# A two-layer hybrid decoder trunk: SBUF buffers moved to 2 KB multiples, inputs laid out before the launch, the inverse's products alternated

## The chip, the cores and the metric

The kernel runs on one core of one Trainium2 chip. Its time is device microseconds, from one launch; the runs of a kernel are given by their median. Each core has TensorE (PE in the profile, its weight loads as PEld), VectorE (DVE), ScalarE (ACT), GpSimd (POOL), SyncE (SP, which only issues DMAs here) and 16 DMA engines. [...]

## The reference

256 positions of width 2048 go through two layers. Each layer normalises its input, projects it to 7692 columns, feeds three mixers from them and projects their gated outputs back:

```python
h = rms_norm(x, norm_w[l])                       # (256, 2048)
u = h @ w_in[l]                                  # (2048, 7692), float32
y_conv = conformer_conv(...)                     # 512 wide: GLU, 31-tap conv, LayerNorm, swish, 512 x 512
y_gdn  = gated_deltanet(...)                     # 6 heads of 128: 4-tap conv, chunked delta rule
y_att  = dilated_attention(...)                  # 12 heads of 64
x = x + concat(gated y_conv, y_gdn, y_att) @ w_out[l]
```

A last RMSNorm gives the output. All parameters are float32, and the result must be close to float32 accuracy. The delta rule needs, for each head and chunk, the inverse of a unit lower-triangular matrix (`triangular_solve` of the reference).

## The kernel before

**Products in three terms.** Weights and activations are split into a high part in float32r (a cheaper float32 for TensorE) and the low rest, and each product is high·high + low·high + high·low. For the weights ACT copies `raw` to `whi` and DVE subtracts to get `wlo`; for the activations `HT[0]` and `HT[1]` are the two parts of the transposed normalised input, each 16 blocks of 128 x 256, and `YT[0]`, `YT[1]` those of the mixers' outputs. `unit` (L453) issues the three products of one block. A matmul loads 128 columns of one operand as weights and streams the other one past them: with `chan` the weights are the stationary operand and 256 columns of `HT` or `YT` stream; otherwise 384 to 512 columns of `whi` or `wlo` stream. `last_unit` (L462) is used for the last 256 output columns, where `YT` is stationary and `HT`, which then holds weights, streams.

**Order.** The kernel is written as tasks; `Plan.run` gives each step a cost and an earliest start, and writes every engine's instructions in the order of its own model. On the chip each engine keeps that order. `load_weights` is one stream of chunks on SP's queue (two 128-row blocks of weights for each, four `raw` buffers, three `whi` and three `wlo`), `split_weights` follows, and `project` runs the jobs one after the other on two pairs of PSUM banks (`ACC`). Everything else of the mixers is put between the units of the projections.

**The start.** `load_x` loads `x` by columns between the first weight chunks (`X_BEFORE`); `norm_block`, `norm_half` and `norm_128` transpose each 128 x 128 piece on TensorE (32 transposes, L230) and split the result out of PSUM into `HT`. `square_sums` has ACT form the sums of squares of the same pieces; `finish_norm` makes 1/rms of them, which the evacuation of the projections applies, so the first products do not wait for it. `setup` loads small parameters as rows and turns them by TensorE transposes too (`turn`, L339): four for each layer.

**The inverse.** `inverse` inverts 32 x 32 blocks on DVE and then merges them: 12 products of 32 x 32 for each of several steps, then 64 x 64 ones, all plain float32 (L223; such a product shows as two matmul records in the profile). Each step's result is copied out of PSUM by DVE before the next step reads it. The two halves of the 128 partitions, named by `prs`, go through the steps one after the other, and so do the two groups of six heads in the 64 x 64 steps. The planner puts units of a projection between the steps.

**Placement.** In the built program `HT` and `YT` start 128 bytes past a multiple of 2 KB in each partition; `raw`, `whi` and `wlo` start 1856 bytes past one, and their second blocks of 384 columns 1344 bytes past one.

## Time and profile before

| | us |
|---|---|
| median of 3 runs | 997.62 |
| lowest and highest run | 996.41, 998.58 |
| the profiled execution | 998.17 |
| its span, first to last instruction | 996.5 |
| TensorE busy in the span | 983.1 (99%) |
| VectorE busy | 749.7 (75%) |
| ScalarE busy | 551.9 (55%) |
| GpSimd busy | 48.6 (5%) |

The granted clock was 0.997 of the higher level over the whole span. The profiled execution is 0.55 us above the median. A busy TensorE is not TensorE at its peak: matmuls overlap, so what one costs is read from how many start in a stretch (the pitch), not from the duration of one, and the waits show where it stood still. The chain of work that ended last follows, step by step, what released each instruction; its pieces give a start, a length and a count, and the length over the count is the pitch.

### The profile page before, as it was taken

What the parts mean: (1) busy time and instruction counts of PE and PEld (TensorE: products, weight loads), DVE (VectorE), ACT (ScalarE), POOL (GpSimd) and SP (SyncE); (2) the same over time, 40 slices, a digit from 0 to 9 for tenths busy, and PEclk for the clock granted to TensorE, in tenths of its full rate; (3) what the DMA queues carried; (4) which work ended last, traced back from release to release, by engine and by line L of the source; (5) the groups of instructions that cost most, each with busy time, mean ns of one, the idle gap of its engine ahead of it and who ended that gap; (6) DMA issues with size and microseconds to landing.
All of it is one profiled execution on the core that took longest, in us unless ns stands there. A gap on an engine that the chain in (4) does not pass through costs nothing.

```text
span 996.5 us, 19159 instructions
## 1 busy us (share of the span) xinstructions
PE 983.1 (99%) x7299; PEld 958.3 (96%) x7299; DVE 749.7 (75%) x1511; ACT 551.9 (55%) x1085; POOL 48.6 (5%) x70
## 2 busy tenths in 40 slices
PE   8999999999999999999999999999999999999996
PEld 7999999999999989999899999999999999999996
DVE  6587699988899666655557767999888987666672
ACT  7665345544676674454455633554447777545452
POOL 1000200200010000000000020002000101000000
PEclk9999999999999999999999999999999999999998
DMA  8665566644444635776766655666444456466772
GB/s 269 172 213 174 158 182 184 195 147 129 143 144 143 190 117 169 219 223 223 231 183 182 201 167 171 182 184 189 137 141 130 142 174 207 122 185 219 226 247 87
DMA packets 116585, 176.91 MB, mean 178 GB/s; under 512 B 8458, under 2 KB 97356, under 8 KB 116492
## 3 DMA queue, kind: packets, MB, share of 16 engines
q1 hardware_dynamic: 114572, 171.88, 56.4%
q0 software_dynamic: 1632, 3.02, 1.2%
q8 instruction: 57, 0.93, 0.4%
q10 hardware_dynamic: 288, 0.79, 0.2%
q14 instruction: 36, 0.29, 0.1%
HBM read 170.67 MB, written 4.98 MB: 176 GB/s over the span
## 4 chain that ended last, share of the span: by engine, by line
PE 97%; issue 1%; DMA 1%; DVE 0%; ACT 0%; SPq 0%; POOLq 0%; POOL 0%; DVEq 0%; ACTq 0%
PE acc L453 86%; PE mix L223 6%; PE mix L230 3%; DMA b<-in_x 1%; PE acc L462 1%; PE mix L751 0%; DVE wlo L190 0%; ACT b L182 0%; SPq L408 0%; DVE b L197 0%; SPq L390 0%; PE mix L339 0%; ACT whi L182 0%; POOLq L1300 0%; POOL rstd L239 0%
## 5 line engine op out<-in xcount | busy, mean ns | idle before, releaser
L182 ACT ACTIVATE whi<-raw 128x768 fp32r<-128x768 f32 (+4 forms) x389 | 339.7, 873 | 375.5 <-PE acc L453 319.0
L190 DVE TENSOR_TENSOR wlo<-raw,whi 128x768 fp32r<-128x768 f32 (+4 forms) x389 | 385.5, 991 | 193.0 <-ACT whi L182 186.2
L453 PE MATMUL acc<-HT,whi 128*128 128x256 f32 x2304 | 413.2, 281 | 0.0
L453 PEld LDWEIGHTS acc<-HT,whi 128*128 128x128 f32 x2304 | 352.0, 188 | 1.6 <-issue 1.5
L453 PE MATMUL acc<-HT,wlo 128*128 128x256 f32 x1152 | 321.7, 279 | 0.0
L453 PE MATMUL acc<-whi,HT 128*128 128x384 f32 (+1 forms) x1024 | 271.2, 346 | 0.0
L453 PEld LDWEIGHTS acc<-HT,wlo 128*128 128x128 f32 x1152 | 216.0, 188 | 0.0
L453 PEld LDWEIGHTS acc<-whi,HT 128*128 128x128 f32 x1024 | 179.8, 188 | 1.9 <-issue 1.0
L453 PE MATMUL acc<-wlo,HT 128*128 128x384 f32 (+1 forms) x512 | 172.6, 337 | 0.0
L453 PE MATMUL acc<-whi,YT 128*128 128x384 f32 (+2 forms) x640 | 162.8, 338 | 0.0
L453 PEld LDWEIGHTS acc<-whi,YT 128*128 128x128 f32 x640 | 114.2, 187 | 3.0 <-ACT whi L182 0.2
L453 PE MATMUL acc<-wlo,YT 128*128 128x384 f32 (+2 forms) x320 | 107.9, 337 | 0.4 <-DVE wlo L190 0.4
L187 DVE SCALAR_TENSOR_TENSOR b<-b,dw,b 128x255 f32<-128x255 f32 (+29 forms) x240 | 104.3, 461 | 0.2
L453 PEld LDWEIGHTS acc<-wlo,HT 128*128 128x128 f32 x512 | 96.1, 188 | 0.0
L453 PEld LDWEIGHTS acc<-wlo,YT 128*128 128x128 f32 x320 | 60.0, 187 | 2.2 <-DVE wlo L190 0.7
L230 PE MATMUL mix<-ident,b 128*128 128x128 f32 x312 | 51.2, 276 | 3.0 <-DMA b<-in_x 2.6
L182 ACT ACTIVATE b<-mix 128x256 f32<-128x256 f32 (+3 forms) x95 | 38.6, 422 | 19.1 <-PE mix L223 10.0
L187 DVE SCALAR_TENSOR_TENSOR b<-b,cw,b 128x255 f32<-128x255 f32 (+2 forms) x108 | 48.6, 473 | 0.0
L223 PE MATMUL mix<-b,b 128*128 128x128 f32 (+5 forms) x456 | 47.8, 285 | 0.4 <-ACT b L182 0.4
L230 PEld LDWEIGHTS mix<-ident,b 128*128 128x128 f32 x312 | 37.7, 140 | 8.3 <-DMA b<-in_x 3.5
L223 PEld LDWEIGHTS mix<-b,b 128*128 128x128 f32 (+3 forms) x456 | 38.0, 161 | 7.5 <-issue 2.7
L187 DVE SCALAR_TENSOR_TENSOR b<-b,b 128x256 f32<-128x256 f32 (+3 forms) x62 | 31.3, 510 | 2.7 <-ACT b L182 2.6
(149 smaller groups left out, 648.0 us busy)
## 6 DMA issues: line engine op xcount, KB each, us to landing
raw<-in_w_in SPq DMA_DIRECT2D x240, 384.0 KB, 3.1
raw<-in_w_in SPq DMA_DIRECT2D x48, 512.0 KB, 3.5
raw<-in_w_out SPq DMA_DIRECT2D x64, 384.0 KB, 3.8
raw<-in_w_out SPq DMA_DIRECT2D x12, 512.0 KB, 5.4
raw<-in_w_in SPq DMA_DIRECT2D x15, 396.0 KB, 4.6
raw<-in_conf_pw_w SPq DMA_DIRECT2D x4, 512.0 KB, 3.7
raw<-in_w_out SPq DMA_DIRECT2D x8, 256.0 KB, 4.2
b<-in_x SPq DMA_DIRECT2D x6, 256.0 KB
```

The costliest lines, as they stand in the source:

```text
L182: lambda: nc.scalar.activation(out_, in_, func, bias=bias, scale=scale, **kw))
L187: lambda: nc.vector.scalar_tensor_tensor(out_, a, s, b, op0=op0, op1=op1))
L190: return ("dve", 70 + _free(out_) / 0.96, lambda: nc.vector.tensor_tensor(out_, a, b, op=op))
L223: nc.tensor.matmul(o, a, b, start=f[0], stop=f[1])
L230: nc.tensor.transpose(o, a, ident)
L453: nc.tensor.matmul(o, w, m, start=first and i == 0 and not (chan and t % 2), stop=last and i == 2, skip_group_check=chan)
L462: nc.tensor.matmul(acc[t][:, :n], YT[w][:, k, s], HT[m][:, k, :n], start=k == 0 and i == 0, stop=k == KB - 1 and i == 2)
```

## The change

Four edits come together.

- **Inputs laid out before the launch.** `w_in`, `conf_pw_w` and `w_out` are stored so that the two 128-row blocks of a chunk lie side by side: each partition's part of a chunk of 384 columns is one run of 3072 bytes and no longer two of 1536. A transposed copy of `x` (`x_t`) is added beside `x`. All small parameters come as one 128 x 237 array for each layer (`params`), with channels on partitions.
- **The start.** `load_xt` and `norm_xt` read `x_t` and split it straight into `HT`, without transposes; `load_x` still loads `x`, now in eight pieces behind chunks 8 to 15, and for `square_sums` alone. `setup` becomes one DMA (on ACT's queue for layer 0, on SP's for layer 1), one activation and two small DVE steps.
- **The inverse.** The two `prs` halves of a 32 x 32 step are issued in one group, alternating; the second 64 x 64 product of one group of heads alternates with the first of the other.
- **Placement.** `lncs` and `ropes` and two pads (`PAD`) are allocated so that `HT`, `YT`, `PTs`, `raw`, `whi`, `wlo` and the 1024-wide buffers start on multiples of 2 KB; the 768-wide ones alternate between 0 and 1024 bytes past one. The residues of all slices that the projections use are then multiples of 512 bytes.

```diff
+PAD = (32, 16)
+    lncs = cp.tile([128, 384], F32, name="lncs")
+    ropes = cp.tile([128, NT, 32], F32, name="ropes")
+    cp.tile([128, PAD[0]], F32, name="pad0")
     HT = [cp.tile([128, KB, S], F32R, name=f"HT{i}") for i in range(2)]
...
+    cp.tile([128, PAD[1]], F32, name="pad1")
     HALF = [cp.tile([128, NT], F32, name=f"half{l}") for l in range(DEPTH)]
...
-    X_PIECES = [(256 * i, 256) for i in range(4)] + [(1024, 512), (1536, 512)]
-    X_BEFORE = {0: 0, 2: 1, 3: 2, 4: 3, 5: 4, 7: 5}
+    X_PIECES = [(256 * i, 256) for i in range(8)]
+    XT_BEFORE = {0: (0, 1), 1: (1, 1), **{i: (2 * i - 2, 2) for i in range(2, 9)}}
+    X_BEFORE = {8 + j: j for j in range(len(X_PIECES))}
...
-        yield from turn(MISC[l][:, 0:16], [(col(norm_w), 16)], cost=0.0 if l == 0 else 100.0)
+        yield ("dma", 200.0 if l else 0.0, lambda: (nc.sync if l else nc.scalar).dma_start(PAR[l], params[l]))
         yield ("set", misc_ready[l])
...
+    def load_xt(k0, m):
+
+        buf = yield ("get", S768)
+        yield ("dma", 128 * m * S * 4 / 330.0, lambda: nc.sync.dma_start(
+            buf[:, :m * S], bass.AP(tensor=x_t.tensor, offset=x_t.offset + k0 * S, ap=[[KB * S, 128], [1, m * S]])))
+        plan.spawn(norm_xt(k0, m, buf), 2)
+
+    def norm_xt(k0, m, buf):
+        yield ("wait", misc_ready[0])
+        for b in range(m):
+            k = k0 + b
+            yield from split(HT[0][:, k, :], HT[1][:, k, :], buf[:, b * S:(b + 1) * S], PAR[0][:, k:k + 1])
+            yield ("set", h_ready[0][k])
+        yield ("put", S768, [buf])
...
-            for p, (a, b) in enumerate(prs):
-                yield mms(*((psx[b, hc * 32:hc * 32 + 32], Lh(hc)[a, b], T3[a, hc, :]) for hc in range(HC)))
+            yield mms(*((psx[b, hc * 32:hc * 32 + 32], Lh(hc)[a, b], T3[a, hc, :]) for hc in range(HC) for a, b in prs))
...
+            yield mms(*(m for hc in range(HC) for m in third(hc)))
...
+            yield mms(*(down(0, j) for j in range(H)))
+            yield cpy(Xs[b, hs[0], :], h3(psx[b, :H * 64], 64))
+            yield mms(*(m for j in range(H) for m in (down(1, j), up(0, j))))
```

What this moves. On TensorE at the program's start, before (`mix` and `acc` are PSUM, `b` the loaded `x` or parameters):

```order
L309 MATMUL mix_118<-ident,ones 128x128 x10
L339 MATMUL mix_121<-ident,b_0_110 128x16
L230 MATMUL mix_120<-ident,b_0_85 128x128 x2
L309 MATMUL mix_119<-ident,ones 128x128 x5
L230 MATMUL mix_120<-ident,b_0_85 128x128 x2
L230 MATMUL mix_118<-ident,b_1_86 128x128 x4
L453 MATMUL acc_122<-whi_79,HT_71 128x396
L453 MATMUL acc_122<-whi_79,HT_72 128x396
```

And of the change:

```order
L316 MATMUL mix_121<-ident,ones 128x128 x10
L316 MATMUL mix_122<-ident,ones 128x128 x5
L453 MATMUL acc_125<-whi_82,HT_74 128x396
L453 MATMUL acc_125<-whi_82,HT_75 128x396
L453 MATMUL acc_125<-wlo_85,HT_74 128x396
```

The products of the first job now follow the 15 warm-up transposes at once; the transposes of `b` are gone here and between the later units of that job.

On ACT where the second copy of `x` is read (the last block of `HT`, then squares into `JUNK`, each with a copy of a weight chunk between), of the change:

```order
L191 ACTIVATE JUNK,ssq_153<-b_9_97 128x256 x2
L191 ACTIVATE whi_84<-raw_78 128x792
L191 ACTIVATE HT_74<-b_8_96,par_147 128x256
L191 ACTIVATE JUNK,ssq_153<-b_10_98 128x256 x2
L191 ACTIVATE whi_82<-raw_79 128x768
L191 ACTIVATE JUNK,ssq_153<-b_11_99 128x256 x2
L191 ACTIVATE whi_83<-raw_80 128x768
```

One pair of squares of 256 columns stands before each weight chunk, eight times; before, squares of 256 and 512 columns stood there in twelve single steps.

On TensorE in the inverse of layer 0, before (one step of the 32 x 32 merge and the two that follow):

```order
L223 MATMUL mix_119<-b_1_105,b_9_94 32x32 x6
L223 MATMUL mix_119<-b_1_105,b_11_96 32x32 x6
...
L223 MATMUL mix_118<-b_0_104,inv_115 32x32 x12
L223 MATMUL mix_118<-inv_115,b_0_104 32x32 x12
```

And of the change:

```order
L232 MATMUL mix_124<-b_1_108,b_9_97 32x32 x12
L232 MATMUL mix_124<-b_1_108,b_8_96 32x32 x12
...
L232 MATMUL mix_122<-b_0_107,inv_118 32x32 x2
L232 MATMUL mix_122<-inv_118,b_0_107 32x32
L232 MATMUL mix_122<-b_0_107,inv_118 32x32 x2
L232 MATMUL mix_122<-inv_118,b_0_107 32x32
```

A layer's 60 small products of 32 x 32 stand in two groups instead of four, and its 24 of 64 x 64 in three instead of four, with other partitions in turn inside a group.

## Rows read from the trace of the kernel before

**Rows 1.** Page, part 1: busy us, share of the span and instructions of each engine.
```profile
PE 983.1 (99%) x7299; PEld 958.3 (96%) x7299; DVE 749.7 (75%) x1511; ACT 551.9 (55%) x1085; POOL 48.6 (5%) x70
```

**Rows 2.** Waits of TensorE, the longest: us in total, times, longest us.
```profile
PE mix L230 <- DMA b<-in_x: 2.6, 2, 1.7
```

**Rows 3.** The chain in pieces: start us, length us, what, count.
```profile
100.46 43.11 PE acc L453 x366
143.79 6.13 PE acc L453 x54
...
429.25 16.97 PE acc L453 x96
446.88 16.64 PE acc L453 x96
...
977.06 5.75 PE acc L462 x48
```

**Rows 4.** Page, part 2: granted clock of TensorE in 40 slices, in tenths.
```profile
PEclk9999999999999999999999999999999999999998
```

**Rows 5.** TensorE's instructions by shape: count | busy us, mean ns.
```profile
L453 PE MATMUL acc<-HT,whi 128*128 128x256 f32 x2304 | 413.2, 281 | 0.0
...
L453 PE MATMUL acc<-whi,HT 128*128 128x384 f32 x896 | 237.0, 345 | 0.0
...
L453 PE MATMUL acc<-whi,YT 128*128 128x384 f32 x512 | 131.7, 338 | 0.0
```

**Rows 6.** Instructions of the first 11 us: start us, length us, engine, what.
```profile
0.80 0.43 SPq L390 DMA_DIRECT2D b<-in_x  x1
...
3.91 0.28 PE L339 MATMUL mix<-ident,b 16*128 16x16 f32 x1
...
4.84 0.53 ACT L182 ACTIVATE whi<-raw 128x396 fp32r<-128x396 f32 x1 [0.42 <-DMA raw<-in_w_in]
...
7.74 0.61 PE L453 MATMUL acc<-whi,HT 128*128 128x396 f32 x2
...
10.13 0.98 DVE L190 TENSOR_TENSOR wlo<-raw,whi 128x792 fp32r<-128x792 f32 x1 [0.36 <-ACT whi L182]
```

**Rows 7.** Stretches of 4 us; the last three: clock, DMA share, GB/s.
```profile
4.00:8.00 4.00, 2.32 (x15) 2.04 (x16) 2.26 (x5) 2.09 (x5) 0.13 (x1) 1.00 0.84 253
8.00:12.00 4.00, 3.04 (x18) 2.41 (x18) 1.87 (x4) 2.61 (x5) 0.00 (x0) 1.00 1.04 365
```

**Rows 8.** The chain in the first 30 us, columns as in rows 3.
```profile
12.40 2.17 PE acc L453 x12
14.57 0.87 PE mix L230 x8
...
29.44 0.11 PE mix L339
```

**Rows 9.** ACT's squares and weight copies after the first job's products: start, length.
```profile
22.50 0.42 ACT L182 ACTIVATE JUNK<-b 128x256 bf16<-128x256 f32 x1
22.82 0.19 ACT L182 ACTIVATION_READ_ACCUMULATOR JUNK<-b 128x1 f32 x1
...
25.46 0.83 ACT L182 ACTIVATE whi<-raw 128x768 fp32r<-128x768 f32 x1
```

**Rows 10.** The chain in layer 0's inverse, columns as in rows 3.
```profile
209.75 0.87 PE mix L223 x24
210.62 2.28 PE acc L453 x12
212.89 1.53 PE mix L223 x48
...
224.35 0.84 PE mix L223 x12
```

**Rows 11.** TensorE inside that inverse: start us, length us, what, count.
```profile
213.48 0.21 PE L223 MATMUL mix<-inv,b 32*32 32x32 f32 x1
...
213.60 0.82 PE L223 MATMUL mix<-inv,b 32*32 32x32 f32 x21
```

## The prediction

> **What bounds the kernel now.** I read the page's busy times first, then TensorE's waits, then the pieces of the chain. TensorE is busy 983.1 us, 99% of the span [rows 1], and its largest wait is 2.6 us in all, for pieces of `x` [rows 2]. The other engines wait for it. So an edit is worth what it takes off TensorE's own stream, and nothing else unless a cover breaks.

> What the stream costs is its pitch. 366 products of 256 columns take 43.11 us, 117.8 ns each; 54 others, of the same tiles and the same shape, take 6.13 us, 113.5 ns each; the 48 of the last job, also 256 columns, take 5.75 us, 119.8 ns each [rows 3]. For 384 columns two neighbouring stretches give 176.8 and 173.3 ns [rows 3]. [...] The 2304 products of 256 columns with `whi` go with half as many with `wlo`, 3456 in all, and the 896 and 512 of 384 columns with 704, 2112 in all [rows 5]. At 117.8 ns and at 175 ns (the middle of the two) they are 407 and 370 us, 777 of 996.5. One ns of pitch on all of them is 5.6 us; that is the size of what the placement can do either way.

> **The change part by part.**

> **The start.** Before, the first product starts at 7.74 [rows 6], and the first job's 96 products of 396 columns end where the transpose at 29.44 stands [rows 8]. Twelve of them take 2.17 us, 180.8 ns each [rows 8], so 96 need 17.4 us; the other 4.3 us after 7.74 are the 28 transposes of `x` that stand between them (8 take 0.87 us, 108.75 ns each [rows 8], so 3.0) and 1.3 us of stops. After: `x_t` is first on SP's queue. Before, the first `x` was issued at 0.80, and what SP issued right after it, `norm_w`, was turned by TensorE at 3.91 [rows 6]; `params` leaves on ACT's queue at the time of the first `x`. So ACT's split of block 0 can start near 4.1; `raw`, which landed by 4.84 [rows 6] and is now issued one place earlier, is copied behind it in 0.53 us [rows 6], and the first product stands at about 5.2. Two blocks last 12 x 0.181 = 2.2 us, to 7.4. The next pair of blocks needs 1.46 MB to have come in all (0.12 of parameters, 0.13 + 0.20 twice, 0.26 + 0.41), which at 253 to 365 GB/s [rows 7] from about 2.0 us is 6.0 to 7.8; with two splits, a copy and 0.98 us of DVE [rows 6] TensorE stops for about 1.5 us. From there a pair takes 0.67 MB, 1.8 us at 365 GB/s, against 2.2 us of products, and TensorE no longer waits. The job ends at 5.2 + 17.4 + 1.5 = 24.1 instead of 29.4: 5.3 less; I take **5.0**, with bounds 3.5 (the transposes alone, with four of them before 7.74) and 6.5 (no stop).

> **The parameters.** Of eight `setup` transposes two stand in that stretch; the six others cost 0.11 us of chain each [rows 8]: **0.7**. The two scaled copies on DVE are a few tenths of a us, and DVE is busy 75%: they are covered.

> **The second copy of `x`.** 2.1 MB more go over SP's queue behind chunks 8 to 15; each chunk with its piece is 0.66 MB, 1.8 us at 365 GB/s [rows 7], against 18 x 117.8 ns = 2.12 us of products. SP issues each piece ahead of a weight chunk, so the chunk queued behind it is what could be late. ACT has to do 0.83 us of copy and two squares of 0.42 + 0.19 us [rows 9], 2.05 us for the same 2.12. Both covers are thin but the three `whi` buffers lie ahead; cost nothing, and 8 x 0.2 = 1.6 us if ACT falls 0.2 us behind each time. 1/rms comes later than before, but nothing needs it until the third job asks for the first one's banks, about 17 us of products after the first job's end.

> **The weights' layout.** TensorE waits for no weight transfer in the trace [rows 2], so longer runs give it nothing: 0 here, some tenths inside the start.

> **The inverse.** In one layer the 32 x 32 steps stand in the chain as 0.87, 1.53, 0.87 and 0.87 us and the 64 x 64 ones as four of 0.84, of which rows 10 show one of each length [rows 10]: 7.5 us. Each step also makes the units that follow dear: 12 products of 384 take 2.28 us [rows 10] instead of 12 x 174 = 2.09, 0.2 us for each of eight groups. After, five groups, so 3 x 0.2 us less for certain. Whether alternating halves overlap, the trace shows at one place only: where the products of one PSUM half run into those of the other, six starts stand between 213.48 and 213.60 [rows 11], about 20 ns each against 0.87 / 24 = 36 ns for those in a row [rows 10]. If that held for all, the 120 records of 32 x 32 would fall from 4.1 to about 2.3 us and the middle 64 x 64 group from 1.7 to about 0.9. Sum for a layer 0.6 to 3.2, for both 1.2 to 6.4; I take **5**, nearer the overlap, since the products there are of the same kind [rows 11].

> **The placement.** No row shows these tiles on a 2 KB multiple. The rows nearest: within one job the streamed block lies alternately 128 and 1152 bytes past one, the weights at four places 512 bytes apart, and the pitch of the 366 does not care; and 113.5 against 117.8 is seen with the very same buffers, on both sides of one pair of transposes. So the pitch looks like a state that TensorE falls into after an interruption, not like something of the address. I take 0. The bounds: down to 113.5 and 173.3 ns everywhere, 3456 x 4.3 + 2112 x 1.7 = 18.5 us less, and below that to 108.75 ns for 256 columns (the transposes, the least that anything with 128 columns of weights takes) and 108.75 + (173.3 - 113.5) = 168.6 for 384, 31.3 + 13.5 = 45 us less; up to 119.8 and, in the same ratio, 179.7, which is 6.9 + 9.9 = 17 us more.

> [...]

> The sum: 5.0 + 0.7 + 5 = 10.7 off the profiled 998.17 gives 987.5. That execution is 0.55 us above the median of the runs, so I forecast **987** as the median.

> **The rivals.**

> *Aligned operands stream faster.* For it: 384 columns minus 256 is 59.8 ns, and the shortest 256-column pitch is 113.5, so something beyond the columns is paid for in every product, and by an amount that varies; starts off a boundary may be that. Against it: residues 512 bytes apart do not differ. By the bounds above 968.5 to 942; its middle, 955. [...]

> *Aligned operands stream slower.* The one job in which streamed and loaded operand have the same residue (both 128, `HT` and `YT`) is the slowest, 119.8 ns [rows 3]; after the change every pair has the same residue modulo 512. If the two reads of TensorE disturb each other there, every 256-column product goes to 119.8 and the 384 ones up to 179.7: 987 + 7 to 987 + 17, that is 994 to 1004. It is slower than before from about 11 us of pitch on, 2 ns for each product.

> *The change does not do what it says off the placement:* no overlap in the inverse (+3.8), ACT late behind the second `x` (+1.6), the start at its lower bound (+1.5): 994.

> **How the numbers follow.** A time within 0.2% of 997.62 (995.6 to 999.6) is about what a measurement of this kernel cannot tell from no change. Forecast, 982 to 992: 0.45, all faster. Faster streams, 942 to 970: 0.35, all faster. Slower streams, 994 to 1004: 0.14, of which 0.04 within the bound and 0.10 slower. Edits that do little, 991 to 997: 0.06, of which 0.02 within the bound. So faster 0.84, same 0.06, slower 0.10. The range 944 to 1001 leaves out about the lower fifth of the faster streams, with what may lie below them, and the upper part of the slower ones.

> **What would show it.** In the profile after: no L230 transposes before the first job's end, that end near 24 us; TensorE's waits no longer naming `x`, but one of 1 to 2 us for a chunk below 10 us; two groups of 32 x 32 products in each layer, at about 20 ns a record if they overlap and 32 to 36 if not; and above all long pieces of the chain at 117.8 ns for 256 columns and 173 to 177 for 384. Pieces near 109 to 113 or near 120 prove the placement part wrong, and with it the forecast by 5.6 us for each ns. A wait for `whi` between 24 and 45 us would show the second copy's cover broken.

## The result and the profile after

The kernel after takes 989.74 us (median of 4 runs, 989.46 to 989.92) against 997.98 for the kernel before in the same comparison: ratio 0.992, 95% interval 0.9902 to 0.9937, so 8.2 us faster. The profiled execution took 989.68 us, its span 988.0. The forecast was 987 us, its own case 982 to 992; that is right in time and sign. The time is partly luck, though, since two errors nearly cancel: the inverse gave 8.1 us where I took 5, and the placement, which I took at 0, costs 5 to 6.

The page's first part (busy us, share, instructions) and the clock in 40 slices, to be held against [rows 1, 4]:

```profile
PE 976.4 (99%) x7259; PEld 954.8 (97%) x7259; DVE 749.7 (76%) x1519; ACT 550.8 (56%) x1079; POOL 48.4 (5%) x70
...
PEclk9999999999999999999999999999999999999999
```

TensorE is still 99% busy, and this row has its granted clock at 9, 90% or more, in every slice, so the 8 us lie in what TensorE does. (For the first 7.65 us the row has no record behind it; the start, below, comes back to them.) Forty instructions are gone: 32 transposes of `x` and eight of the parameters. Next its waits (us in total, times, longest us), which answer to [rows 2]:

```profile
PE mix L316 <- POOL pw_neg L321: 1.6, 1, 1.6
PE mix L232 <- DVE PTs L206: 0.6, 1, 0.6
PE acc L453 <- DVE wlo L199: 0.4, 1, 0.4
PE mix L232 <- DVE inv L212: 0.3, 1, 0.3
PE acc L453 <- ACT whi L191: 0.3, 1, 0.3
```

The wait for `x` is gone. The longest one left, 1.6 us for the first constants, stood in the kernel before too (1.6, at L309); the others are small. Now the chain in pieces (start us, length us, what, count), the rows that answer to [rows 3]:

```profile
95.79 43.92 PE acc L453 x366
139.93 6.48 PE acc L453 x54
...
421.65 16.65 PE acc L453 x96
438.95 16.65 PE acc L453 x96
...
968.12 5.78 PE acc L462 x48
```

The 366 products take 120.0 ns each, where before they took 117.8; the 54 also 120.0, where before 113.5. The two stretches of 384 columns now both stand at 173.4, where before one was at 176.8. The last job is about where it was, at 120.4 (119.8 before). So the pitch did move with the placement, up for 256 columns and down for 384 columns with `YT`. Two stretches are no sum, so here is the time from each product's start to the next one's, added up from the traces by form:

| form (products) | before, us | after, us |
|---|---|---|
| 256 columns of `HT` past `whi`, `wlo` (3456) | 411.4 | 418.6 |
| 256 columns of `YT` past `whi`, `wlo` (96) | 11.5 | 11.7 |
| 384 columns of `whi`, `wlo` past `HT` (1344) | 245.2 | 245.2 |
| 384 columns of `whi`, `wlo` past `YT` (768) | 136.1 | 133.8 |
| 512 columns past `YT` (96) | 22.5 | 21.9 |
| 256 columns of `whi`, `wlo` past `YT` (96) | 10.9 | 11.5 |

That is 5.1 us more on these products. The rest of the change must therefore have given about 13 us, not 10.7.

The start, from the timeline of TensorE (start us, length us, engine, what), where the first job's products of 396 columns give way to the second job's of 256:

```profile
24.77 0.34 PE L453 MATMUL acc<-wlo,HT 128*128 128x396 f32 x1
24.95 0.40 PE L453 MATMUL acc<-HT,whi 128*128 128x256 f32 x2
```

The first job ends at 24.95, where before it ended just ahead of 29.44 [rows 8]. Its first products are slower than the later ones, as two records of one form show:

```profile
6.50 0.53 PE L453 MATMUL acc<-wlo,HT 128*128 128x396 f32 x1
...
10.67 0.34 PE L453 MATMUL acc<-wlo,HT 128*128 128x396 f32 x1
```

From the second to the sixth product the starts stand 328 to 332 ns apart; from 7.8 us on, where nothing is waited for, 175 to 184. 396 columns in 330 ns are 1.2 for each ns, in 180 ns 2.2. The trace's own record of the granted clock begins at 7.65 us, and the page counts the time ahead of it as full; the record holds 1.0 up to 983.86 us and 0.5 after that, with TensorE idle. The trace before shows the same step within one form: its record begins at 4.81 us, and the starts of its 128 x 128 transposes, where they follow one another, stand 213 to 214 ns apart up to 4.82 us and 109 to 110 from there to 5.37. That the clock was lower ahead of the record is read from these pitches and not recorded. Where the record begins is not part of the change: it lies between 4.81 (before) and 10.84 us (the old start in the new kernel) in the traces of the whole kernels here.

And the inverse of layer 0 in the chain, where before stood the rows of [rows 10]:

```profile
206.68 0.88 PE mix L232 x48
207.56 3.32 PE acc L453 x18
210.88 0.88 PE mix L232 x72
...
215.26 0.84 PE mix L232 x12
216.10 2.29 PE acc L453 x12
218.39 0.84 PE mix L232 x24
219.23 3.33 PE acc L453 x18
222.56 0.84 PE mix L232 x12
```

Forty-eight records of 32 x 32 now take 0.88 us and 72 take 0.88 us, where 24 took 0.87; 24 records of 64 x 64 take the 0.84 us that 12 took. The groups add up to 4.28 us instead of 7.5.

### The profile page after: what moved, and what is told of

It is laid out like the page before. It is cut to its first block, busy times and chain, and to the rows that moved or that the text cites. A ratio compares the mean times of both kernels' runs of the same rounds, so it can differ in the third digit from the quotient of the medians.

```text
span 988.0 us, 19060 instructions
## 1 busy us (share of the span) xinstructions
PE 976.4 (99%) x7259; PEld 954.8 (97%) x7259; DVE 749.7 (76%) x1519; ACT 550.8 (56%) x1079; POOL 48.4 (5%) x70
## 4 chain that ended last, share of the span: by engine, by line
PE 96%; DMA 1%; DVE 1%; issue 1%; ACT 0%; SPq 0%; POOLq 0%; POOL 0%; DVEq 0%; ACTq 0%
PE acc L453 86%; PE mix L232 6%; PE mix L239 3%; DMA raw<-in_w_out 1%; PE acc L462 1%; DMA raw<-in_w_in 1%; DVE wlo L199 0%; PE mix L752 0%; ACT whi L191 0%; DVE b L196 0%; DVE HT L199 0%; SPq L367 0%; DVE inv L212 0%; ACT HT L191 0%; SPq L409 0%
## 5 line engine op out<-in xcount | busy, mean ns | idle before, releaser
L453 PE MATMUL acc<-HT,whi 128*128 128x256 f32 x2304 | 420.1, 284 | 0.0
L453 PEld LDWEIGHTS acc<-HT,whi 128*128 128x128 f32 x2304 | 359.1, 192 | 1.5 <-issue 1.5
L453 PE MATMUL acc<-HT,wlo 128*128 128x256 f32 x1152 | 325.8, 283 | 0.0
L453 PEld LDWEIGHTS acc<-HT,wlo 128*128 128x128 f32 x1152 | 220.7, 192 | 0.0
L196 DVE SCALAR_TENSOR_TENSOR b<-b,par,b 128x255 f32<-128x255 f32 (+20 forms) x348 | 153.6, 465 | 0.3
L191 ACT ACTIVATE b<-mix 128x384 f32<-128x384 f32 (+3 forms) x96 | 39.6, 424 | 20.5 <-PE mix L232 12.7
L239 PE MATMUL mix<-ident,b 128*128 128x128 f32 x280 | 45.8, 274 | 0.0
L239 PEld LDWEIGHTS mix<-ident,b 128*128 128x128 f32 x280 | 34.2, 140 | 3.7 <-issue 1.3
L191 ACT ACTIVATE b<-b,stat 128x128 f32<-128x128 f32 (+1 forms) x68 | 29.1, 442 | 6.0 <-DVE stat L206 5.9
```

The costliest lines, as they stand in the source:

```text
L191: lambda: nc.scalar.activation(out_, in_, func, bias=bias, scale=scale, **kw))
L196: lambda: nc.vector.scalar_tensor_tensor(out_, a, s, b, op0=op0, op1=op1))
L239: nc.tensor.transpose(o, a, ident)
L453: nc.tensor.matmul(o, w, m, start=first and i == 0 and not (chan and t % 2), stop=last and i == 2, skip_group_check=chan)
```

## The experiments

Two theories stood against each other on the placement. **B** is the prediction's: the pitch is a state that TensorE falls into after an interruption and does not hang on the address. **A**, the rival that the trace after points to: the addresses of the streamed and the loaded operand against each other set it. Three parts of the change (inverse, start, layouts) had to be priced apart as well. Each run is held against the 989.74 us of the kernel after. The kernel before, run again beside each of them, stood at 997.8 us, and at 996.9 beside the last two shifts; so differences of under 1 us are not told apart here.

### The placement undone, and the placement alone

```diff
-PAD = (32, 16)
+PAD = (64, 448)
```

> The kernel after with other pads alone (64 and 448 words for 32 and 16): HT and YT start 128 and raw, whi, wlo 1856 bytes past a multiple of 2 KB, as in the kernel before. Theory A (the pitch follows from the start addresses of the two operands against each other): 256 columns go back from 120.0 to 117.8 ns, 384 columns of whi past YT from 173.3 to 176.7, 512 from 226.7 to 233.3; 3456 x 2.2 ns less, some 3 us more for the wide ones, so about 985.5 (983 to 988). Theory B (the prediction's: a state after an interruption, not the address): the pieces stay at 120.0 and 173.3 and the time at 989.7 (988.7 to 990.7).

The other way round, the kernel before with the placement alone:

```diff
+    lncs = cp.tile([128, 384], F32, name="lncs")
+    ropes = cp.tile([128, NT, 32], F32, name="ropes")
+    cp.tile([128, PAD[0]], F32, name="pad0")
     HT = [cp.tile([128, KB, S], F32R, name=f"HT{i}") for i in range(2)]
...
-    lncs = cp.tile([128, 384], F32, name="lncs")
-    ropes = cp.tile([128, NT, 32], F32, name="ropes")
...
+    cp.tile([128, PAD[1]], F32, name="pad1")
     HALF = [cp.tile([128, NT], F32, name=f"half{l}") for l in range(DEPTH)]
```

> The kernel before with the placement alone: lncs and ropes moved ahead of HT and the two pads, so that every large buffer stands where the kernel after has it; loads, start and inverse as before. Theory A: 256 columns at 120.0 ns, 384 with YT at 173.3, about 4 us slower than before, 1002 (1000 to 1005). Theory B: 998 (997 to 999), with pieces at 117.8.

Measured: 983.97 us (ratio to before 0.9856, 0.9843 to 0.987) for the first, 1003.05 us (1.0054, 1.004 to 1.0068) for the second. Both lie in the ranges of theory A. So the placement costs 5.8 us in the new kernel and 5.2 in the old one, and theory B, by which nothing should have moved, falls. The chain of the first shows the pitch, 117.8 ns again:

```profile
95.40 43.11 PE acc L453 x366
```

and that of the second, the old kernel with the new residues, 120.0 ns:

```profile
101.49 43.92 PE acc L458 x366
```

### A scan of the start addresses

Two small kernels with nothing but rows of products, each row with one pair of start residues:

```python
for i, (n, a, b) in enumerate(plan_rows()):
    acc = accs[i % 2]
    a, b = a // 4, b // 4
    for j in range(REP):
        m, s = 512 * (j % 3) * 2 + a, 512 * (j % 4) + b
        nc.tensor.matmul(acc[:, :n], sta[:, s:s + 128], mov[:, m:m + n], start=j == 0, stop=j == REP - 1)
```

> A kernel that computes nothing of the reference: rows of 12 float32r products each into one PSUM bank, 128 columns loaded and 256, 384 or 512 streamed, no other engine at work. For 256 columns every pair of start residues in steps of 32 bytes modulo 512, streamed and loaded, in a shuffled order and twice; for 384 and 512 columns steps of 64 bytes of one of them; some finer and wider steps (4 to 48, 512 to 1792 bytes). Theory A: the pitch of 256 columns hangs on the difference streamed minus loaded modulo 512 alone: 120.0 at 0, 117.8 at 320, 113.3 at 192; 384 columns 173.3 at 0 and up to 176.7 elsewhere, 512 226.7 at 0 and 233.3 at 192. Theory B: one pitch for all pairs, or values that go with what ran just before and not with the pair. Theory C: each residue by itself matters (both on a boundary fast or slow), not the difference.

> A kernel that computes nothing of the reference, as the first scan: rows of 18 float32r products, for 256 columns the loaded operand 0 to 252 bytes past the streamed one in steps of 4, for 384 and 512 columns 0 to 240 in steps of 16 with the streamed one at 0 and at 128, shuffled, three times. Theory A: the same values for the same difference whatever the streamed residue, 113.3 for 256 columns at 64 and 192 and in their neighbourhood, and 384 columns least at 192, near 173; a state shows as two values for one difference, never as one value for all. Theory B: the values differ between repeats by as much as between differences.

Each row's pitch is taken from the starts of its last products (seven of 12, ten of 18). The first scan, 256 columns, 64 rows for each difference of loaded minus streamed start modulo 256 (16 streamed residues, two loaded ones 256 bytes apart, twice):

| difference, bytes | lowest | median | highest, ns |
|---|---|---|---|
| 0 | 118.2 | 119.8 | 120.7 |
| 32 | 117.5 | 118.0 | 119.2 |
| 64 | 113.3 | 113.3 | 117.8 |
| 96 | 117.0 | 117.7 | 120.0 |
| 128 | 117.7 | 118.7 | 120.0 |
| 160 | 118.8 | 120.0 | 120.0 |
| 192 | 113.3 | 117.8 | 117.8 |
| 224 | 115.8 | 116.7 | 120.0 |

Theory A holds in its main point: the difference sorts the pitch, whatever the streamed residue is by itself. Of the scatter of all 512 rows (a variance of 3.7 ns squared) 0.9 is left within groups of one difference, but all 3.7 within groups of one streamed, or of one loaded, residue. (The theory counts streamed minus loaded; the table has the sign turned.) It was off in one: the period is 256 bytes and not 512 (differences of 64 and of 320 have the same median, 113.3). Theory C, that each residue by itself matters, falls. Theory B is not all wrong: at 64 and at 192 there are two steady values, 113.3 and 117.8, for the very same pair (51 of 64 rows at the lower one with 64, 8 of 64 with 192). The kernel before stood at 192 for `HT` past `whi`, which is why it showed both 117.8 and 113.5 with the same buffers [rows 3].

The fine scan (three rows each, streamed operand on a boundary) at the differences used below, and the wide products of 384 and 512 columns at the opposite ones, to the nearest step of 16 (there `whi` streams and `YT` is loaded, so the sign turns over):

| difference | 256 columns, ns | | difference | 384 columns, ns | 512 columns, ns |
|---|---|---|---|---|---|
| 0 | 120.0, 120.0, 120.0 | | 0 | 173.3, 173.3, 173.3 | 226.7, 226.7, 226.7 |
| 64 | 117.8, 117.8, 117.8 | | 192 | 173.3, 173.3, 173.3 | 233.3, 228.9, 228.9 |
| 76 | 113.3, 113.3, 113.3 | | 176 | 173.3, 173.3, 173.3 | 230.7, 229.9, 229.9 |
| 192 | 113.3, 117.8, 117.8 | | 64 | 174.7, 173.3, 176.7 | 233.3, 233.0, 233.6 |
| 204 | 123.7, 120.3, 123.7 | | 48 | 173.3, 173.3, 173.3 | 233.3, 233.4, 233.2 |

Part of the fine scan's expectation missed: 113.3 was to stand at 64, at 192 and around them, and there it came in one of these six rows and in none of the next steps (60, 68, 188, 196). No row of 256 columns is below 113.3 in either scan. And 0, which the change chose, is the best for 512 columns, one of the best for 384 in this scan and one of the worst for 256.

### Shifting the weights against the activations

By the scan the buffers are to stand apart, not together. First 64 bytes, by the second pad alone, with everything behind it (`raw` too):

```diff
-PAD = (32, 16)
+PAD = (32, 32)
```

> The kernel after with the second pad 64 bytes larger (32 words for 16): HT and YT stay on 2 KB multiples, raw, whi and wlo start 64 bytes past one. Theory A (the scan's: the difference loaded minus streamed modulo 256 sets the pitch; at 64 the steady pitch of 256 columns is 113.3 ns, after some entries 117.8): 3456 x 6.7 ns less than after if the faster value holds throughout, 967; 3456 x 2.2 less, 982, if the slower one does; 384 columns of whi past HT or YT, at 192, stay at about 173. Theory C (the boundary itself matters: an operand on a 2 KB multiple is best or worst whatever the other does): between after and the old residues, 984 to 990.

Measured 972.61 us (0.9754, 0.9741 to 0.9767), between the two ends of theory A. The chain shows both steady values in one kernel, 113.4 ns in the first of these pieces and 117.8 in the second:

```profile
93.87 41.51 PE acc L453 x366
...
570.09 44.52 PE acc L453 x378
```

Counted six in a row at a time, about 1800 of the products of `HT` stand at 113 ns and 1200 at 118. Then 76 bytes, where the fine scan has one value only, meant to shift `whi` and `wlo` alone, inside slightly larger tiles (`OFF` is 19 words):

```diff
-    WHI = Slots([wp.tile([128, 1024], F32R, name=f"whi{i}") for i in range(3)])
-    WLO = Slots([wp.tile([128, 1024], F32R, name=f"wlo{i}") for i in range(3)])
+    WHI = Slots([wp.tile([128, 1056], F32R, name=f"whi{i}")[:, OFF:OFF + 1024] for i in range(3)])
+    WLO = Slots([wp.tile([128, 1056], F32R, name=f"wlo{i}")[:, OFF:OFF + 1024] for i in range(3)])
```

> The kernel after with whi and wlo alone shifted, by 76 bytes against HT and YT (19 words into slightly larger tiles; raw, HT and YT stay on 2 KB multiples). Theory A (the difference sets the pitch, and at 76 the scan has one steady value, 113.3 ns in all three rows, where 64 has two): nearly all products of 256 columns at 113.3 to 113.6, also the stretches that stand at 117.8 with 64; 1212 of those counted there times 4.4 ns, 5.3 us less than with 64: 967 (965 to 969), 384 columns at 173 to 174. Theory B (which of two values holds is a matter of what ran before, not of the difference): some 40% of the products stay at 117.8 and the time at 972.6.

Measured 966.83 us (0.9696, 0.9682 to 0.9709), the time that theory A gave, and the piece that stood at 117.8 is at 113.4 too:

```profile
93.33 41.55 PE acc L454 x366
...
566.80 42.86 PE acc L454 x378
```

But the edit does not do what its text says. A tile of 1056 words is 4224 bytes, 16.5 times 256, so in the built program `whi0`, `whi2` and `wlo1` stand 76 bytes past `HT` modulo 256, and `whi1`, `wlo0` and `wlo2` stand 204 past it: 1924 of the 3456 products at 76 and 1532 at 204, each unit with its `whi` at one and its `wlo` at the other. Where no other work comes between, both kinds stand at 113.8 ns in the mean. By the fine scan's rows for 204, 120.3 to 123.7, those 1532 alone should have cost 11 to 16 us more, so the hit at 967 is partly luck. Where two differences alternate, the rows of one difference do not give the pitch.

All six buffers at 76 came with the same shift in the kernel before, by 35 words in tiles of 1088 (17 times 256 bytes), with nothing else of the change:

> The kernel before with whi and wlo alone shifted by 140 bytes (35 words), so that they stand 76 bytes past HT and YT modulo 256; nothing else of the change. Theory A: 256 columns from 117.8 to 113.4 ns, 3456 x 4.4 = 15.2 us, and 384 columns with YT from 176.7 to 173.3, 768 x 3.3 = 2.5: 980 (978 to 983). Theory B (the old buffers' pitch is not of the address): 998.

Measured 980.27 us (0.9831, 0.9816 to 0.9846), in the range of theory A: 16.6 us less than the kernel before beside it, where 17.7 were expected. The 366 products are at 113.4 ns there as well:

```profile
98.04 41.49 PE acc L456 x366
```

And the difference at which the scan was slowest, 51 words in the kernel after, again in tiles of 1088 words, so that all six buffers stand at 204:

> The kernel after with whi and wlo alone shifted by 204 bytes (51 words), the difference at which the fine scan had its slowest rows for 256 columns: 123.7, 120.3 and 123.7 ns, by their mean 122.6. Theory A (the difference sets the pitch, for worse as for better): pieces of 256 columns at 120.3 to 123.7, 3456 x 2.6 ns = 9 us slower than after, 998.7 (991 to 1003). Theory C (a shift off the 2 KB multiple is what helps): as fast as with 76 bytes, 967.

This one missed: 983.51 us (0.9864, 0.9847 to 0.988), 6 us faster than after where 9 us slower was expected. Theory C's 967 missed as well. The chain shows three values in one kernel, 113.4 ns (366), 119.9 (72) and 123.2 (63):

```profile
96.10 41.49 PE acc L456 x366
...
529.00 7.76 PE acc L456 x63
...
559.62 8.63 PE acc L456 x72
```

Counted in the same way, about 1300 products stand at 113 or 114, about 1300 at 120 or 121 and about 500 at 123. The scan had found two of the three. So the steady values that turn up go with the difference, which of them a stretch takes is settled by something else, and a scan of three rows does not show them all. What that is, the entry into the stretch (the return to the products after other work) or the products that alternate in it, no run settled.

The last job is a control inside every kernel: its `YT` and `HT` stand at a difference of 0 whatever is done to `whi` and `wlo`, and in the traces of all twelve whole kernels its products start 119.6 to 120.0 ns apart.

### The inverse

The kernel after with the inverse's products in the order of before; the diff is the hunk of the change on `inverse`, turned round:

```diff
-            yield mms(*((psx[b, hc * 32:hc * 32 + 32], Lh(hc)[a, b], T3[a, hc, :]) for hc in range(HC) for a, b in prs))
+            for p, (a, b) in enumerate(prs):
+                yield mms(*((psx[b, hc * 32:hc * 32 + 32], Lh(hc)[a, b], T3[a, hc, :]) for hc in range(HC)))
...
```

> The kernel after with the inverse's products in the order of before (the halves one after the other, the two groups of heads too), all else as after. Theory A (products of 32 x 32 in different quarters of the array overlap, as the steps of the trace after add up: 4.3 us in a layer for 7.5 before): both layers together 6 to 8 us slower than after, 996 to 997.5. Theory B (only fewer re-entries into the projection, three per layer at 0.2 us): 1.2 us slower, 991.

Measured 997.83 us, 8.1 slower than after: theory A. The chain of its layer 0 has the old lengths back:

```profile
207.44 0.87 PE mix L232 x24
208.31 2.28 PE acc L453 x12
210.59 1.53 PE mix L232 x48
```

### The start and the layouts

`x` loaded once and transposed as before, all else as after:

```diff
-    X_PIECES = [(256 * i, 256) for i in range(8)]
-    XT_BEFORE = {0: (0, 1), 1: (1, 1), **{i: (2 * i - 2, 2) for i in range(2, 9)}}
-    X_BEFORE = {8 + j: j for j in range(len(X_PIECES))}
+    X_PIECES = [(256 * i, 256) for i in range(4)] + [(1024, 512), (1536, 512)]
+    X_BEFORE = {0: 0, 2: 1, 3: 2, 4: 3, 5: 4, 7: 5}
...
+        plan.spawn(norm_block(0, j, (c0, n), [xs[:, t] for t in range(NT)], nsq0[j], pool, [buf], sums_from=16000.0), 2)
...
```

> The kernel after with the start of before: x loaded once, in six pieces between the first weight chunks, and transposed by TensorE; parameters, weights' layout, inverse and placement as after. By the prediction's step the start is worth 5.0 us (3.5 to 6.5): 994.7, with the first job ending near 29 us again. If the 5.7 us that the placement and the inverse leave of the whole come rather from the parameters' and the weights' layouts, under 992.

Measured 992.45 us (992.18 to 993.51), 2.7 slower than after: less than the 3.5 to 6.5 expected, and more than the under 992 of the other reading. Its first job ends where that of before did, by the timeline of TensorE:

```profile
29.15 0.34 PE L432 MATMUL acc<-wlo,HT 128*128 128x396 f32 x1
29.33 0.40 PE L432 MATMUL acc<-HT,whi 128*128 128x256 f32 x2
```

So the new start gains 4.4 us on the first job. By the starts of the same numbered products in both traces it is 6.4 at the 625th product, 4.4 to 4.6 from the 801st to the last and 3.8 over the span; the profiled execution of this kernel is 1.1 above its own median, which leaves 2.7. In this trace the clock record begins at 10.84 us, and its first products, too, stand 328 to 332 ns apart; in the kernel before they stood at about 180, and yet the first job ends within 0.1 us of the same place.

The weights as the reference has them, two runs of 1536 bytes for a chunk in each partition:

```diff
-            src = bass.AP(tensor=wt.tensor, offset=wt.offset + base + (k // 2) * 256 * n + (k % 2) * n,
-                          ap=[[2 * n, 128]] + ([[256 * n, m // 2]] if m > 2 else []) + [[1, min(m, 2) * n]])
-            chunks.append((src, m, n, k if keep else None))
+            chunks.append((w[k * 128:(k + m) * 128, c0:c0 + n], m, n, k if keep else None))
```

> The kernel after with w_in, conf_pw_w and w_out as the reference has them, so that a chunk of two blocks is two runs of 1536 bytes in each partition; all else as after. By the prediction's step 0 on the whole and some tenths at the start: 989.7 to 990.5. If transfers bound the start (TensorE stops below 10 us), 2 us or more slower: over 991.5.

Measured 990.45 us (990.1 to 991.26), 0.7 slower than after and as expected; a difference of this size is not clear of noise. The weights' layout is worth little: no wait of TensorE names a transfer. The chain of the kernel after runs through two, one at the start and one of `w_out`, and a copy of a weight chunk on ACT follows each:

```profile
3.12 4.95 DMA raw<-in_w_in
...
938.38 5.88 DMA raw<-in_w_out
```

The parameters as rows, turned by TensorE:

```diff
-        yield ("dma", 200.0 if l else 0.0, lambda: (nc.sync if l else nc.scalar).dma_start(PAR[l], params[l]))
+        yield from turn(MISC[l][:, 0:16], [(col(norm_w), 16)], cost=0.0 if l == 0 else 100.0)
...
+        yield from turn(CWT[l], [(conv_qkv_w[l].rearrange("j (c p) -> (j c) p", p=128), 72)])
...
```

> The kernel after with the small parameters loaded as rows and turned by TensorE as before, eight transposes, four DMAs and more a layer; x_t, inverse, weights' layout and placement as after. By the prediction 0.7 us: 990.4. By what the other undone parts leave of the whole (8.3 less the sum of 8.1, 2.7 and 0.7, plus the placement's 5.5): 2.2 us, 992.

Measured 995.09 us (993.91 to 995.97), 5.4 slower than after: both expectations missed. Eight transposes of 0.11 us are 0.9. Most of the rest is not the parameters themselves: with eight more tasks the planner writes another order, and that order stops TensorE once for 2.0 us, at 365 us, between the input projection of layer 0 and the first products of `YT`. Its waits have a line that neither kernel shows (columns as above):

```profile
PE mix L240 <- ACT b L192: 2.0, 1, 2.0
```

Over the span TensorE gets out of its products into small work 154 times instead of 149 and stands still for 5.0 us instead of 1.7 after its first instruction. About 2 us more are lost between the 385th and the 625th product (by their starts in the two traces), beside a different order of small groups there; which of its pieces costs them was not tried apart. Nor was the planner's order held fixed while the parameters changed, so that the order is the cause is argued from these two places and not shown.

## Why the prediction was right, point by point

- **What bounds the kernel:** right. TensorE is busy 99% after as before, and every gain or loss showed on its own stream. "About 5.6 us for each ns of pitch" was too simple: the widths went opposite ways, so 2.2 ns on the 256-column products cost about 7 us and the 384-column ones with `YT` gave 2.3 back.
- **The start, 5.0 taken (3.5 to 6.5):** first product at 4.70, not 5.2; the job's end at 24.95, not 24.1; 4.4 us gained there. The step that was off is the stop: the first 24 products take 7.2 us from 4.70 to 11.93, where 24 x 0.181 are 4.3, so TensorE loses 2.9 us below 12 us and not 1.5. By the starts about 1.2 of the 2.9 are pace, the first products at 328 to 332 ns that the sum left out, 1.3 are three stops, and the rest are longer first gaps after them. The pace does not set the end, though: in five other traces with the same start and layouts the clock record begins at 4.95 to 6.20 us, and their 25th product starts at 11.9 to 12.3 as well, behind longer stops. A reading was off too: of the 32 transposes of `x` before, eight and not four stood ahead of the first product, so 24 and not 28 lay behind it, 2.6 us and not 3.0. At the end of the program 3.8 us of it are left in the profiled executions and 2.7 in the medians.
- **The parameters, 0.7 taken:** mis-sized. 5.4 us by undoing them, about 4 of which go, as far as the traces show, with the other order that the planner makes of the tasks. Undone one at a time, the parts (8.1, 2.7, 0.7, 5.4, less 5.8) come to 11.1, not 8.2; they do not add up; that each undone part moves the plan as well is the likely reason.
- **The second copy of `x` and the weights' layout, 0 each:** right. No wait of TensorE stands between 24 and 60 us in the trace after, so the thin covers on ACT and SP's queue held, and undoing the layout cost 0.7 us, which is not clear of noise. The second copy was not undone by itself.
- **The inverse, 5 taken (1.2 to 6.4):** 8.1. The mechanism was right, overlap of products in different partitions; the record is cheaper than estimated: 120 records in 1.76 us, 14.7 ns each, where the one row of before suggested 20. By groups that is 3.2 us a layer, with three re-entries of 0.2 us 3.8, for both 7.6.
- **The placement, 0 taken:** wrong, and the step that failed is an inference. From "113.5 and 117.8 with the very same buffers" I concluded that the pitch is "not something of the address". What follows from it is only that the address does not settle it alone; the part on a stretch taking one of several values was right. The other observation, that places 512 bytes apart do not differ, was true and empty: the period is 256, so those places are the same one.
- **The rivals:** the one whose mechanism happened, beside the forecast, is "aligned operands stream slower", and for the reason given, equal residues as in the last job. For 256 columns it was right (120.0 where it said 119.8), at a price of 5 to 6 us where it said 7 to 17. For 384 columns, where it said up to 179.7 "in the same ratio", it was wrong: 173.3 to 173.4. "Aligned operands stream faster" was wrong for 256 columns and right, by 2.3 us, for 384 with `YT`. No row of 256 columns in these runs is as short as the 108.75 ns that its lower bound took from the transposes, and the least, 113.3, took another placement than this change.

The sum that the runs support: about 8 for the inverse, 3 to 4 for the start, under 1 for the layout, less 5 to 6 for the placement; that leaves 1 to 2 for the parameters as they stand in this plan, an estimate by what is left of 8.2 and not a measured part.

## What to carry to other kernels

Where TensorE is the bound, read its pitch by stretches, not by form: a chain piece's length over its count shows tenths of a nanosecond, and 4.4 ns (117.8 to 113.4) on 3456 products are 15 us. Where one shape shows several pitches, move one operand by some tens of bytes and look again; equal residues for everything is a choice like any other, and here a poor one (23 us slower than with the weights' buffers at 76 and 204 bytes). Check in the built program that every buffer of a rotation stands where the edit means it to. A result that agrees with a forecast does not confirm its terms: undo each part once.
